# Query-tile order of the last stick-breaking head and of the second sparse group reversed in a two-layer attention trunk

## The chip, the cores and the metric

The kernel runs on one core of a Trainium2 chip (trn2). The metric is device time in microseconds (us), lower is better. The engines are TensorE (PE; its weight loads are PEld), VectorE (DVE), ScalarE (ACT), GpSimd (POOL) and SyncE (SP), which only starts transfers here. POOL and ACT start transfers too.

## The reference, cut to what matters

Two layers, each on 1024 tokens of width 1024. A normalised input goes through one wide projection; two attention mixers read the result; both are gated, projected, merged and added to the residual.

```
h = rms_norm(x, norm_g) * (1 + scale) + shift
sb_q, sb_k, sb_v, sb_z, n_q, k_c, v_c, k_s, v_s, k_w, v_w, n_z, n_g, m_a, m_b = split(h @ w_in)
a = stick_breaking_attention(sb_q, sb_k, sb_v)         # 8 heads, causal
b = native_sparse_attention(...)                       # 8 query heads in 2 groups, causal
a = a * silu(sb_z);  b = b * silu(n_z)
y = sigmoid(m_a) * (a @ w_proj_a) + sigmoid(m_b) * (b @ w_proj_b)
x = x + gate * (y @ w_out)

def stick_breaking_attention(q, k, v):                 # per query tile i of 128 rows
    z = q[tile i] @ k[:tile end].T * scale
    log_keep = where(strict, log_sigmoid(-z), 0)
    between = reverse_cumsum(log_keep) - log_keep
    w = where(strict, exp(log_sigmoid(z) + between), 0)
    out[tile i] = w @ v[:tile end]
...
```

Both mixers are causal, so a query tile near the end of the sequence reads more keys than one near its start.

## The kernel before, in words

Each layer runs four stages: `early` (the first projections), `nsa` (sparse attention), `sb` (stick-breaking attention) and `output`. `nsa` and `sb` work in query tiles `m` = 0 to 3 of 256 tokens; a tile has two halves `x` of 128. Tile `m` of `sb` reads 256m + 128 and 256m + 256 keys in its halves, so tile 0 is the smallest and tile 3 the largest.

`nsa` goes through eight steps `n`: group `g = n // 4`, tile `m = n % 4`. A step has a compressed-branch job and four pair jobs (two head pairs `hp`, two halves `x`). `sb` goes through 32 jobs: eight heads, four tiles each, tiles always from 0 to 3. Each job has a part A (scores and what VectorE and ScalarE make of them: for `sb` two sigmoids into C and E, a running product over C, E times C) and a part B (transposes of E into `tr`, a split into a high and a low half `wh`, `wl`, the products `av` with V, and `merge`). `run_jobs` writes part A of a job between the steps of part B of the job before.

Into these two stages the kernel mixes projection work of its own layer ("fill": 14 groups of 96 matmuls of 512 columns, written by `queue_projections`). `budgets` works out how much of it goes into each slot: what VectorE needs in the slot beyond what TensorE needs, and an equal share of the rest. The tile framework then orders each engine's instructions by the order in the program and by what it takes to be ready, so an instruction of a later stage can stand ahead of one of an earlier stage in an engine's queue.

Transfers around the ends of the stages:

- In the last pair job of a group (`m == 3 and hp == 1 and x == 1`) `nsa` calls `load_kv` for the next group or, after the second, `sb_first`, which writes what is left of the stick-breaking projections and then calls `sb_load(0)` (K by SP into `kk`, q and V by ACT). The buffers of `kk` are shared with the sparse keys, two in all, so the load of K waits for the last scores that read the sparse keys.
- At the end of a job of an odd head, `finish_pair` (L996 to L998) loads the gate rows `szl` (one buffer), multiplies them into the output tile `o` of two heads and stores it from SP to `AD`, rows of that head pair, columns of that tile.
- `output` takes `AD` back in two halves of 512 tokens: half 0 is tiles 0 and 1, half 1 is tiles 2 and 3. `load(half)` starts three transfers per half on POOL (L1462): row blocks 4 to 8 (the sparse heads), 0 to 3 (heads 0 to 5), and 3 to 4 (heads 6 and 7). Each block of 128 rows is then split into `acthi` (ACT, L130) and `actlo` (DVE, L131).
- `load(0)` is written ahead of everything else in `output`. `y_unit` then makes two sums in the two buffers of `proj`: first over blocks 4 to 8, then over 0 to 4, 12 matmuls each, block 3 last. A buffer comes free when VectorE has multiplied it by the gate rows `gt` (L1532), which POOL loads for the first units (L1528). `load(1)` is tied behind the gate loads of the second unit.

The lines that say the order of the first unit:

```
for k0, k1 in ((4, 8), (0, 3), (3, 4)):
    nc.gpsimd.dma_start(lo[:, k0:k1, :].bitcast(F32), self.AD[k0 * P:k1 * P, half * 512:half * 512 + 512]
...
for x, ks in ((1, range(4, 8)), (0, range(0, 4))):
```

Of the kernel before, what the change touches and what calls it, by code (L numbers as in the profile page):

```python
# [87 lines left out]
class Trunk:  # L88
# [186 lines left out]
    def budgets(self):  # L275

        def pe(n):
            return max(0.112, 0.000455 * n)  # L280

        def ve(n):
            return 0.15 + 0.00104 * n

        def parts(nk):
            return [b - a for a, b in self.cuts(nk)]

        def splits(blocks):
            return sum(ve(128 * min(4, blocks - b)) for b in range(0, blocks, 4))

        def nsa(i):
            nk, nw = 128 * i + 128, min(384, 128 * i + 128)
            blocks = (nk + nw) // 64
            A = (4 * (sum(map(pe, parts(nk))) + pe(nw)), 2 * (sum(ve(n) + 0.1 for n in parts(nk)) + ve(nw) + 0.1))
            B = (pe(128) * blocks + 2 * pe(256) * (blocks // 2 + 1),
                 0.34 + 2 * (0.22 + 0.00053 * nk) + splits(blocks) + ve(256) + ve(512) / 2)
            return A, B

        def cmp(m):
            n = 4 * (8 * m + 8)  # L300
            return (8 * pe(128), 2 * (0.5 + 6 * ve(n) + (2.4 if m >= 2 else 0.0))), (4 * pe(128), ve(512))

        def stick(m):
            ks = (256 * m + 128, 256 * m + 256)
            A = (2 * sum(pe(n) for nk in ks for n in parts(nk)) + 0.08, sum(0.13 + 0.0021 * n + ve(n) for n in ks))
            B = (pe(128) * (4 * m + 3) + 2 * (pe(256) * (2 * m + 1) + pe(128)), splits(4 * m + 3) + 1.5 * ve(256))
            return A, B

        seqs = []
        seq = [cmp(0)]  # L310
        for n in range(8):
            i = n % 4 * 2
            seq += [nsa(i), nsa(i + 1)] + ([cmp((n + 1) % 4)] if n < 7 else []) + [nsa(i), nsa(i + 1)]
        seqs.append((seq, 1.25))
        seqs.append(([stick(m) for _ in range(8) for m in range(4)], 1.16))
        zero = ((0.0, 0.0), (0.0, 0.0))
        out = []
        for seq, per in seqs:
            seq = [zero] + seq + [zero]
            out.append([max(0.0, b[1][1] + a[0][1] - b[1][0] - a[0][0]) * per for b, a in zip(seq[:-1], seq[1:])])  # L320
        rest = (14 * 96 * pe(512) - sum(map(sum, out))) / sum(map(len, out))
        return [[(x + rest) * 0.213 / pe(512) for x in o] for o in out]
# [684 lines left out]
        nc.vector.tensor_tensor(o[a:a + 64], ps[a:a + 64, 0:256], t[a:a + 64], ALU.add)  # L1007


    def nsa_load_kv(self, g):  # L1010
        if g < 2:
            pool = self.kvq_pool
            self.kv[g] = (self.load_stack_k(pool, 1536 + g * 64), self.load_stack_k(pool, 1664 + g * 64),
                          self.load_v(pool, 8 + g), self.load_v(pool, 10 + g))
# [15 lines left out]
    def nsa_load_q(self, n):  # L1030
        if n >= 8:
            return
        g, m = n // 4, n % 4
        q = self.tl(self.kvq_pool, [P, 4, 256], F32R, "q")
        for hl in range(2):
            self.nc.scalar.dma_start(
                q[hl * 64:hl * 64 + 64].bitcast(F32),
                self.QK[hl, 1024 + g * 256:1024 + g * 256 + 256, m * 256:m * 256 + 256]
                .rearrange("(h d) t -> d h t", d=64))
        self.qs[n] = q  # L1040
# [17 lines left out]
    def nsa(self, l):  # L1058
        tc, nc = self.tc, self.nc
        with tc.tile_pool(name=f"nsa{l}", bufs=2, reuse_waits="tile") as pool:  # L1060
            kv, qs, cmp = self.kv, self.qs, {}
            load_kv, load_q = self.nsa_load_kv, self.nsa_load_q

            def cmp_job(n):
                g, m = n // 4, n % 4
                st = {"sel": [None, None], "pg": [None, None]}
                cmp[n] = st
                return ([lambda x=x: self.nsa_cmp(pool, g, m, x, qs[n], st) for x in range(2)],
                        [lambda: None] * 2 + [lambda: self.nsa_cmp_t(pool, st)])

            def pair_job(n, hp, x, st):

                g, m = n // 4, n % 4
                hs = {}
                A, B = [], []
                if hp == 0 and x == 0:
                    A.append(lambda: load_q(n + 1))
                if m == 3 and hp == 1 and x == 1:
                    A.append(lambda: load_kv(g + 1) if g == 0 else self.sb_first())
                for r in range(2):  # L1080
                    A += self.nsa_scores(pool, g, m, hp * 2 + r, r, x, lambda: qs[n], lambda: kv[g], cmp[n], hs)
                B.append(lambda: self.nsa_scale(pool, g, m, hp, x, hs))
                B += self.nsa_av(pool, g, m, hp, x, lambda: kv[g], cmp[n], hs)

                def fin():
                    if x == 0:
                        st["o"] = self.tl(pool, [64, 2, 256], F32, "o")
                    self.nsa_merge(pool, hs["ps"], st["o"][:, :, x * P:x * P + P])
                    if x == 1:
                        self.nsa_finish(pool, st["o"], g * 4 + hp * 2, m)  # L1090
                B.append(fin)
                return A, B

            jobs = [cmp_job(0)]
            for n in range(8):
                for hp in range(2):
                    st = {}
                    for x in range(2):
                        if hp == 1 and x == 0 and n + 1 < 8:
                            jobs.append(cmp_job(n + 1))  # L1100
                        jobs.append(pair_job(n, hp, x, st))
            self.run_jobs(jobs, self.budgets()[0])
# [215 lines left out]
    def sb(self, l):  # L1318
        tc, nc = self.tc, self.nc
        with tc.tile_pool(name=f"sb{l}", bufs=2, reuse_waits="tile") as pool:  # L1320
            qkv = self.qkv

            def job(head, m, st):
                hs = {}
                A, B = [], []
                for x in range(2):
                    A += self.sb_scores(pool, m, x, lambda: qkv[head], hs)

                def begin():
                    if m == 0:  # L1330
                        self.sb_load(head + 1)
                    hs["ps"] = self.tl(self.pav, [P, 512], F32, "av", bufs=1)
                bursts = self.pipeline(pool, self.av_stages(pool, m, lambda: (hs["e", 0], hs["e", 1]),
                                                            lambda: qkv[head][2]), lambda: hs["ps"], True)
                B.append(lambda: (begin(), bursts[0]()))
                B += bursts[1:]

                def fin():
                    if head % 2 == 0:
                        st[m] = self.tl(pool, [P, 256], F32, f"o{m}", bufs=1)  # L1340
                    self.merge(pool, hs["ps"], st[m], head % 2)
                    if head % 2 == 1:
                        self.finish_pair(pool, st[m], head // 2 * 128, m, 512 + head // 2 * 128)
                B.append(fin)
                return A, B

            jobs = []
            st = {}
            for head in range(8):
                for m in range(4):  # L1350
                    jobs.append(job(head, m, st))
            self.run_jobs(jobs, self.budgets()[1])

    def sb_scores(self, pool, m, x, qkv, hs):
# [227 lines left out]
```

## Time and profile before

| what | value |
|---|---|
| median of 3 runs | 2152.11 us (2149.16 to 2154.95) |
| the profiled execution | 2147.3 us, span of its records 2145.5 us |
| TensorE busy | 2085.5 us, 97% of the span |
| VectorE busy | 1583.9 us, 74% |
| ScalarE busy | 1125.3 us, 52% |
| mean granted TensorE clock | 0.994 of full speed |
| fill, matmuls of 512 columns per layer | 1344 |

All stretches are in us from the start of the span. Layer 0 has its `nsa` stage at about 284 to 657, `sb` from there to about 911, `output` to about 1150; layer 1 has `nsa` at 1336 to 1703, `sb` to about 1959 and `output` to the end. A wait named "PE tr <- DVE E" is idle time of TensorE in front of a transpose that needed E.

### The profile page before, as it was taken

To read this page: it belongs to the slowest core of one execution; us is meant where nothing else is said; L and a number is where in the kernel's file an instruction comes from. 1 tells how busy PE (TensorE), PEld (TensorE's weight loads), DVE (VectorE), ACT (ScalarE), POOL (GpSimd) and SP (SyncE) were. 2 spreads that over 40 slices of the span, in tenths; PEclk is the share of its full clock that TensorE was granted. 3 is DMA by queue.
4 is the path that set the end of the run, shared out by engine and by line. 5 is a ranking of instruction groups with operands and counts; after the bars stand their busy time and mean duration, and the time that the engine had idled before them with its cause. 6 is when DMAs were issued, how large, how long until landed. Compare 5 with 4: busy or idle time off the path is not lost.

```text
span 2145.5 us, 36387 instructions
## 1 busy us (share of the span) xinstructions
PE 2085.5 (97%) x12952; PEld 1816.3 (85%) x12952; DVE 1583.9 (74%) x3718; ACT 1125.3 (52%) x2461; POOL 59.7 (3%) x218
## 2 busy tenths in 40 slices
PE   4999999999999999999999999999999999999999
PEld 3899788989888878779899987898898888887899
DVE  6758568888887888866766763888888788887543
ACT  5433146666676666653533422656766666666410
POOL 0200000000000000100011000000000000001000
PEclk8999999999999999999999999999999999999999
DMA  8446934243216545365466464322632454535433
GB/s 308 101 146 188 308 101 122 84 131 113 84 55 159 141 119 143 118 221 168 156 163 171 132 193 143 89 95 80 166 102 65 120 131 123 141 99 183 149 123 104
DMA packets 256150, 297.02 MB, mean 138 GB/s; under 512 B 38888, under 2 KB 201568, under 8 KB 255968
## 3 DMA queue, kind: packets, MB, share of 16 engines
q1 hardware_dynamic: 214992, 250.57, 39.1%
q10 hardware_dynamic: 36432, 29.45, 5.3%
q0 software_dynamic: 4544, 14.68, 2.5%
q8 instruction: 102, 1.67, 0.3%
q14 instruction: 80, 0.66, 0.1%
HBM read 206.28 MB, written 83.89 MB: 135 GB/s over the span
## 4 chain that ended last, share of the span: by engine, by line
PE 79%; DVE 8%; DMA 7%; issue 3%; ACT 2%; SPq 1%; POOL 0%; DVEq 0%; ACTq 0%; POOLq 0%
PE proj L182 17%; PE proj L184 17%; PE proj L186 17%; PE tr L969 7%; PE av L989 5%; PE av L988 4%; PE sc L956 4%; PE sc L957 4%; DVE w L131 1%; DVE C L1372 1%; DMA gt<-MD 1%; DMA ada<-in_ada_w 1%; DMA raw<-in_w_in 1%; DVE E L1373 1%; PE sc L1111 1%
## 5 line engine op out<-in xcount | busy, mean ns | idle before, releaser
L182 PE MATMUL proj<-acthi,w 128*128 128x512 f32 x1312 | 533.6, 407 | 5.6 <-DVE gt L1532 3.6
L184 PE MATMUL proj<-actlo,w 128*128 128x512 f32 x1312 | 534.4, 407 | 0.9 <-DVE actlo L131 0.9
L186 PE MATMUL proj<-acthi,w 128*128 128x512 f32 x1312 | 532.5, 406 | 0.0
L130 ACT CAST w<-raw 128x512 fp32r<-128x512 f32 (+1 forms) x296 | 182.2, 622 | 219.8 <-PE proj L186 133.0
L182 PEld LDWEIGHTS proj<-acthi,w 128*128 128x128 f32 x1312 | 248.6, 189 | 46.9 <-DVE gt L1532 4.8
L131 DVE TENSOR_TENSOR wl<-tr,wh 128x512 fp32r<-128x512 f32 (+2 forms) x408 | 253.4, 638 | 46.7 <-ACT wh L130 44.2
L184 PEld LDWEIGHTS proj<-actlo,w 128*128 128x128 f32 x1312 | 248.8, 190 | 38.2 <-DVE actlo L131 2.4
L186 PEld LDWEIGHTS proj<-acthi,w 128*128 128x128 f32 x1312 | 248.2, 189 | 37.8 <-DVE w L131 0.4
L131 DVE TENSOR_TENSOR w<-raw,w 128x512 fp32r<-128x512 f32 (+1 forms) x296 | 202.2, 689 | 83.6 <-ACT w L130 81.5
L130 ACT CAST wh<-tr 128x512 fp32r<-128x512 f32 (+2 forms) x408 | 216.3, 552 | 72.0 <-PE tr L969 65.5
L182 PE MATMUL proj<-w,acthi 128*128 128x256 f32 (+1 forms) x768 | 220.8, 288 | 4.6 <-ACT G L879 2.2
L186 PE MATMUL proj<-w,actlo 128*128 128x256 f32 (+1 forms) x768 | 220.5, 287 | 0.0
L184 PE MATMUL proj<-w,acthi 128*128 128x256 f32 (+1 forms) x768 | 219.6, 286 | 0.1
L988 PE MATMUL av<-wh,V 128*128 128x256 f32 (+1 forms) x776 | 203.7, 280 | 0.4
L989 PE MATMUL av<-wl,V 128*128 128x256 f32 (+1 forms) x776 | 201.2, 287 | 0.9 <-DVE wl L131 0.5
L1372 DVE TENSOR_TENSOR_SCAN C<-C 128x128 f32<-128x128 f32 (+7 forms) x128 | 173.4, 1354 | 24.5 <-ACT C L1368 23.9
L969 PE MATMUL tr<-ident,E 128*128 128x128 f32 x1152 | 180.8, 276 | 9.1 <-DVE E L1373 6.9
L969 PEld LDWEIGHTS tr<-ident,E 128*128 128x128 f32 x1152 | 140.1, 141 | 42.2 <-DVE E L1373 11.9
L956 PE MATMUL sc<-kk,q 128*128 128x384 f32 (+4 forms) x512 | 174.5, 341 | 0.3
L957 PE MATMUL sc<-kk,q 128*128 128x384 f32 (+4 forms) x512 | 172.6, 337 | 0.0
L989 PEld LDWEIGHTS av<-wl,V 128*128 128x128 f32 x776 | 146.0, 188 | 17.3 <-DVE wl L131 7.0
L988 PEld LDWEIGHTS av<-wh,V 128*128 128x128 f32 x776 | 146.5, 189 | 12.2 <-ACT wh L130 4.5
(241 smaller groups left out, 3896.1 us busy)
## 6 DMA issues: line engine op xcount, KB each, us to landing
raw<-in_w_in SPq DMA_DIRECT2D x168, 256.0 KB, 3.3
ada<-in_ada_w SPq DMA_DIRECT2D x48, 512.0 KB, 5.5
kk<-QK SPq DMA_DIRECT2D x48, 512.0 KB, 8.1
q<-QK ACTq DMA_DIRECT2D x64, 256.0 KB, 4.9
QK<-s SPq DMA_DIRECT2D x32, 512.0 KB, 2.8
MD<-sz SPq DMA_DIRECT2D x64, 256.0 KB, 2.3
QK<-s SPq DMA_DIRECT2D x48, 256.0 KB, 4.3
VD<-s SPq DMA_DIRECT2D x48, 256.0 KB, 2.1
```

The costliest lines, as they stand in the source:

```text
L130: nc.scalar.copy(hi, src)
L131: nc.vector.tensor_tensor(lo, src, hi.bitcast(F32), ALU.subtract)
L182: nc.tensor.matmul(ps, lh, rh, start=(x == 0), stop=False)
L184: nc.tensor.matmul(ps, lh, rl, start=False, stop=False)
L186: nc.tensor.matmul(ps, ll, rh, start=False, stop=(x == n - 1))
L956: nc.tensor.matmul(ps, q, k[:, 0, c0:c1], start=True, stop=False)
L957: nc.tensor.matmul(ps, q, k[:, 1, c0:c1], start=False, stop=not masks)
L969: nc.tensor.transpose(pt[:, x * P:x * P + P], b, self.ident)
L988: nc.tensor.matmul(ps[:, c:d], lhsT, hi[:, a:b], start=(first and x == 0), stop=False, skip_group_check=True)
L989: nc.tensor.matmul(ps[:, c:d], lhsT, lo[:, a:b], start=False, stop=(last and x == n - 1), skip_group_check=True)
L1111: nc.tensor.matmul(ps[:, h], q[:, h, x * P:x * P + P], self.KCS[:, :, g * 64:g * 64 + nn], start=True, stop=True)
L1372: nc.vector.tensor_tensor_scan(rev, rev, rev, 1.0, ALU.mult, ALU.bypass)
```

## The change

The second sparse group takes its tiles in the order 3, 2, 1, 0, and the eighth stick-breaking head too; everything else keeps its order. The two functions that say the order are used by the job lists and by `budgets` alike. The call of `load_kv` and `sb_first` stays in the last pair job of each group, which in the second group is now one of tile 0. No instruction is added or removed; jobs, the projection work between them and the transfers tied to them are placed in another order.

```
@@ budgets
         for n in range(8):
-            i = n % 4 * 2
-            seq += [nsa(i), nsa(i + 1)] + ([cmp((n + 1) % 4)] if n < 7 else []) + [nsa(i), nsa(i + 1)]
+            i = self.nsa_at(n)[1] * 2
+            seq += [nsa(i), nsa(i + 1)] + ([cmp(self.nsa_at(n + 1)[1])] if n < 7 else []) + [nsa(i), nsa(i + 1)]
-        seqs.append(([stick(m) for _ in range(8) for m in range(4)], 1.16))
+        seqs.append(([stick(m) for _, m in self.stick_at()], 1.16))
...
+    @staticmethod
+    def nsa_at(n):
+        return (0, n) if n < 4 else (1, 7 - n)
+
+    @staticmethod
+    def stick_at():
+        return [(h, m if h < 7 else 3 - m) for h in range(8) for m in range(4)]
@@ nsa_load_q, cmp_job, pair_job
-        g, m = n // 4, n % 4
+        g, m = self.nsa_at(n)
...
-                if m == 3 and hp == 1 and x == 1:
+                if n % 4 == 3 and hp == 1 and x == 1:
                     A.append(lambda: load_kv(g + 1) if g == 0 else self.sb_first())
@@ sb
-                    if m == 0:
+                    if m == 0 and head < 7:
                         self.sb_load(head + 1)
...
-            for head in range(8):
-                for m in range(4):
-                    jobs.append(job(head, m, st))
+            for head, m in self.stick_at():
+                jobs.append(job(head, m, st))
```

## Rows read from the trace of the kernel before

**Rows 1.** Stretches: length, busy us (instructions) by engine, granted clock, DMA share.
```profile
284.00:640.00 356.00, 355.54 (x2317) 315.39 (x2316) 287.07 (x894) 227.95 (x549) 1.11 (x7) 1.00 0.32 96
640.00:665.00 25.00, 24.94 (x154) 21.12 (x152) 15.57 (x34) 16.39 (x34) 0.73 (x5) 1.00 0.92 222
665.00:880.00 215.00, 212.09 (x1231) 174.57 (x1231) 181.87 (x244) 138.64 (x306) 5.65 (x57) 1.00 0.47 123
...
903.00:917.00 14.00, 11.13 (x62) 8.60 (x61) 12.79 (x22) 9.29 (x18) 3.63 (x6) 1.00 0.88 297
...
1949.50:1953.50 4.00, 1.55 (x9) 1.20 (x7) 3.62 (x6) 3.95 (x9) 0.00 (x0) 0.81 0.52 172
1953.50:1957.00 3.50, 3.50 (x21) 3.27 (x20) 3.35 (x6) 3.18 (x7) 0.00 (x0) 0.73 0.25 75
```

**Rows 2.** TensorE's waits, 900 to 917 (layer 0): us, times, longest.
```profile
PE tr L969 <- DVE E L1373: 1.5, 1, 1.5
PE proj L182 <- DVE gt L1532: 1.0, 1, 1.0
```

**Rows 3.** TensorE's waits, 1945 to 1980 (layer 1).
```profile
PE tr L969 <- DVE E L1373: 2.5, 1, 2.5
PE proj L184 <- DVE actlo L131: 0.9, 3, 0.4
PE proj L182 <- ACT acthi L130: 0.6, 1, 0.6
PE proj L182 <- DVE gt L1532: 0.2, 1, 0.2
```

**Rows 4.** Timeline of VectorE, layer 1: start, us, instruction, idle before it.
```profile
1949.82 0.69 DVE L131 TENSOR_TENSOR actlo<-actlo,acthi 128x512 fp32r<-128x512 f32 x1 [0.81 <-ACT acthi L130]
1950.43 0.68 DVE L131 TENSOR_TENSOR w<-raw,w 128x512 fp32r<-128x512 f32 x1
1951.03 1.22 DVE L1373 TENSOR_TENSOR E<-E,C 128x1024 f32<-128x1024 f32 x1
```

**Rows 5.** Timeline of TensorE at the end of `sb`, layer 1.
```profile
1948.42 0.40 PE L186 MATMUL proj<-acthi,w 128*128 128x512 f32 x1
1948.65 0.39 PE L182 MATMUL proj<-acthi,w 128*128 128x512 f32 x1
...
1952.30 2.61 PE L969 MATMUL tr<-ident,E 128*128 128x128 f32 x11 [2.45 <-DVE E L1373]
```

**Rows 6.** TensorE's timeline: the last product of `sb` in each layer.
```profile
910.69 0.27 PE L989 MATMUL av<-wl,V 128*128 128x128 f32 x1
...
1958.48 0.27 PE L989 MATMUL av<-wl,V 128*128 128x128 f32 x1
```

**Rows 7.** SP's timeline: the last store to `AD` in each layer.
```profile
914.66 0.32 SPq L998 DMA_DIRECT2D AD<-o  x1
...
1961.24 0.32 SPq L998 DMA_DIRECT2D AD<-o  x1
```

**Rows 8.** POOL's timeline: the load of `AD` that needs that store.
```profile
920.32 0.57 POOL L1462 DMA_DIRECT2D actlo<-AD  x1 [11.06 <-DVE w L131]
...
1966.80 0.57 POOL L1462 DMA_DIRECT2D actlo<-AD  x1 [4.23 <-issue]
```

**Rows 9.** Lines L998 (32 stores) and L1462 (12 loads): issue to landing.
```profile
DMA to landing us min/median/max: 1.7/3.0/5.5
...
DMA to landing us min/median/max: 5.2/8.6/11.0
```

**Rows 10.** DMA issues by size, section 6 and its longer answer: KB, median us to landing.
```profile
kk<-QK SPq DMA_DIRECT2D x48, 512.0 KB, 8.1
...
AD<-o SPq DMA_DIRECT2D x64, 128.0 KB, 2.5
...
actlo<-AD POOLq DMA_DIRECT2D x4, 256.0 KB, 6.9
```

**Rows 11.** Timelines of SP and TensorE, layer 0: first K load, first score of `sb`.
```profile
643.12 0.57 SPq L937 DMA_DIRECT2D kk<-QK  x1
...
652.55 0.23 PE L956 MATMUL sc<-kk,q 128*128 128x128 f32 x1
```

More of the change, by code (lines that the diff above doesn't have):

```diff
@@ L1064, in cmp_job @@
             def cmp_job(n):
-                g, m = n // 4, n % 4
+                g, m = self.nsa_at(n)
                 st = {"sel": [None, None], "pg": [None, None]}
@@ L1071, in pair_job @@
             def pair_job(n, hp, x, st):
-                g, m = n // 4, n % 4
+                g, m = self.nsa_at(n)
                 hs = {}
```

## The prediction

> **What bounds the kernel now.** I read the busy times by stretch first, then TensorE's waits in the stretches where it was not full, then the timelines of the engines at the two stage ends, and last the landing times of the transfers there.
>
> The stretches say that TensorE sets the pace almost everywhere: in the sparse stage of layer 0 it is busy 355.54 of 356 us, and in the 25 us across the change of stage, from sparse to stick-breaking, 24.94 of 25 [rows 1]. In the body of the stick-breaking stage it loses about 3 of 215 us [rows 1]. So reordering jobs inside these stages can win next to nothing there: the same matmuls run, and the projection work already fills the gaps. What there is to win lies where TensorE stands still. At the end of the stick-breaking stage of layer 0 it waits 1.5 us for the last E, and 2.5 us in layer 1 [rows 2, 3]. The reader should see why the second is longer: VectorE, which takes its queue in order, first waits 0.81 us for a block that `output` has loaded, splits it, splits a weight block, and only then multiplies the last, 1024 wide E [rows 4].
>
> The clock makes the second wait dearer. It is granted at 0.81 in 1949.5 to 1953.5 and at 0.73 in 1953.5 to 1957 [rows 1]. A loss of 0.19 over 4 us and of 0.27 over 3.5 us is 1.5 and 1.9 us at the lower of the two levels, 1.2 GHz instead of 2.4, together 3.4 us. TensorE starts again at 1952.30 with 11 transposes that take 2.61 us [rows 5]; about 3.1 of the 3.4 us lie behind that start, so about 1.5 us of work is lost. Before the fall it had stood still. In layer 0, where it stood for 1.5 us, the clock stayed at 1.00 [rows 1, 2].
>
> **The change, part by part.** No instruction is added or dropped; three things move.
>
> *The last jobs of the stick-breaking stage become small.* The last E is 256 wide, not 1024, and its part B has 3 transposes and 6 products, not 15 and 30. This takes away the waits for E: 1.5 + 2.5, and the 1.5 of the clock, 5.5 us in both layers together. The splits of the loaded blocks still stand in VectorE's queue around the last E, so I leave 0.5 us per layer and count −4.5 (ends: 0, if those splits hold up the small E as well, and −5.5). By the formula in `budgets` the last two slots hold 25.7 + 2.4 matmuls of fill before and 9.3 + 4.3 after; the sum over the stages is the same, so this is work moved and not saved.
>
> *The half that `output` needs first is now finished last.* This is the part that costs. Tiles 0 and 1 of heads 6 and 7 are block 3 of half 0. Before, half 1 was the late half, and `output` needs it later. The trace has the whole late chain, for half 1. From the end of the last product, 910.96 and 1958.75 [rows 6], to the store on SP it is 3.7 and 2.5 us [rows 7]: a copy, an addition and the gate product. From the store to the POOL load that needs it, another 5.7 and 5.6 us [rows 8]. Over all 32 stores the landing takes 1.7 to 5.5, median 3.0 [rows 9]. The load of this size takes 6.9 at the median, and no load of that line under 5.2 [rows 9, 10]. Then come the two splits, 0.7 each by the one in [rows 4] (ACT's estimated alike).
>
> For half 0 I take 2.5 to the store, 3.0 to its landing (the median, because the 1.75 MB of the other half need not be in the queues then), 6.0 for the load (between 5.2 and 6.9) and 1.4 for the splits: 12.9 us from the last product until block 3 can be used. Ends: 2.5 + 1.7 + 5.2 + 1.4 = 10.8, and 3.7 + 5.7 + 6.9 + 1.4 = 17.7.
>
> What hides it is the work of `y_unit` without block 3: 12 + 9 matmuls in the first unit. They follow each other every 0.23 us [rows 5], so 4.9 us. The two `proj` buffers allow as many in the second unit, if the engines' queues are written so that it goes ahead; then both buffers hold sums that want block 3 and TensorE must stop. That gives 9.8 us. Some 9 matmuls (2.1 us) will run beside the last small job, an estimate from its 2.5 us of transposes, split and products. So 7.7 us lie behind the last product, or 2.8 if only the first unit is there. The queues do mix later work in (the block split ahead of E in [rows 4] is one case), so I take 7.7: the stall is 12.9 − 7.7 = 5.2 us. It is longer than the one after which the clock fell in layer 1, so I add 1.5 for the clock. Per layer 6.7, for both 13.4 (ends: 3.1 without the clock, 6.2 for both; 17.7 − 2.8 + 1.5 = 16.4, 32.8 for both).
>
> The waits now at the head of `output` fall into this stall: 1.0 for `gt` in layer 0, and 0.9 + 0.6 + 0.2 in layer 1 [rows 2, 3]: −2.7 (ends 0 and −2.7). What queues behind the late load: on POOL it is in front of whatever follows it, which may be the `gt` loads; on ACT and DVE the splits of block 3 are in front of later gate products. If `gt` is caught too, the cover is the 2.8 us.
>
> The Trainium skill, page "DMA: Bandwidth & Descriptors", section "Anatomy of one DMA — SWDGE (gpsimd) path", says that a transfer takes about 2.0 us plus its bytes at 436 GB/s, the first part mostly waiting until the last write is confirmed. Estimated from that page, 128 KB [rows 10] would take 2.3 us and 256 KB 2.6, the chain 2.5 + 2.3 + 2.6 + 1.4 = 8.8, the stall 1.1 a layer without a fall of the clock, and the whole sum −3.0. The trace disagrees for the load, whose shortest is 5.2 [rows 9].
>
> *The sparse stage ends with tile 0.* K of the first stick-breaking head can be loaded only once the last sparse scores are done. Before, 9.4 us passed from that load, 643.12, to the first score, 652.55, with part B of a large job in between and hardly any idle time [rows 1, 11]. Now part B of the last job is small: 8 transposes and 10 products, about 2 us. With the second half's remaining window scores and products and the fill of the slots there (about 5 + 8.4 + 8.5 matmuls by `budgets`, 5.1 us), TensorE has 7 to 9 us of work, against 8.1 us for the landing of a K transfer [rows 10]. More fill can be drawn ahead, but what is drawn there is missing later. I count 1.0 us per layer, +2.0 (ends 0 and 2.4 per layer, which is 9.4 − 7). The order 3, 3, 2, 1 in the middle of the stage costs nothing: TensorE is full there with every size of job [rows 1]; without that cover, as in the stick-breaking body, it would be of the order of 1 us in 70.
>
> **The sum** against the profiled execution: −4.5 − 2.7 + 13.4 + 2.0 = +8.2 us. Its span is 2145.5 us, about 2 us less than its own time and about 7 below the median of the runs; laid on the median of 2152.1 the sum gives 2160. A measurement here tells about 0.3%, 6.5 us, from no change.
>
> **The rivals.**
>
> *The late block is nearly hidden.* If store and load run at their shortest and the second unit goes ahead, the stall is 3.1 a layer without the clock: −4.5 − 2.7 + 6.2 + 2.0 = +1, 2153. For it: the queues carry less when half 1 is not asked for at the same time. Against it: the store that ends the stage took 5.6 us and more in both layers [rows 7, 8]. The page's rule above, with 2149, belongs here.
>
> *The change does nothing that counts.* TensorE is full in the stages [rows 1], and gains and losses at the ends cancel: within 4 us of 2152. The gains for it are in [rows 2, 3]; against it speaks that block 3 of half 0 must come later by construction.
>
> *Faster.* The waits all go, −5.5 − 2.7 = −8.2, and nothing comes in their place: 2144. This is decided at one place: block 3 of half 0 must be usable within 7.7 us of the last product. The shortest pieces in the trace give 10.8, so it needs a load well under 5.2.
>
> *Much slower.* The `gt` loads stand behind the late load on POOL. Then the cover is 2.8, the stall 10.1 + 1.5 a layer, and the sum −4.5 − 2.7 + 23.2 + 2.0 = +18, 2170.
>
> **How the numbers follow.** The forecast has 0.40, much slower 0.12, the nearly hidden block 0.25, the cancelling 0.15, faster 0.08. Slower by over 0.3% (above 2158.6) are the first two, 0.52; within 0.3% the next two, 0.40; faster 0.08. The predicted time is 2160. The range goes from 2148, below the nearly hidden case and most of the cancelling one, to 2172, above the much slower one; outside I leave the faster case and the tail of the long chain, under 2 in 10. The forecast's own range is 2156 to 2166.
>
> **What would show it.** Right: the wait of transposes for E at the end of the stick-breaking stage falls under 1 us in both layers; in its place a wait of 3 us or more of `proj` matmuls for `acthi` or `actlo`, some 3 to 10 us behind the last product; the third load of half 0 on POOL starts 5 us or more after the last product; the clock is below 1.00 in the stretch that follows. Around the K load a wait of scores of 0 to 2.4 us. Wrong: no wait of `proj` for block 3, which would mean that the chain is short or that other work was put in front of it; or a wait for E that stays.

## The result and the profile after

The changed kernel takes 2175.71 us (median of 4 runs, 2169.27 to 2181.55), the kernel before 2151.74 in the runs beside it. The ratio is 1.0116, with a 95% interval from 1.0100 to 1.0131. So the change costs 24.0 us, where 8.2 were forecast; the time lies above the range. The profiled execution takes 2175.72 us and the one of before 2147.3; in this pair the difference is 28.4 us.

The page of the changed kernel, its part on busy times:

```profile
span 2173.9 us, 36400 instructions
...
PE 2095.1 (96%) x12952; PEld 1823.6 (84%) x12952; DVE 1582.7 (73%) x3718; ACT 1125.8 (52%) x2461; POOL 59.0 (3%) x218
```

TensorE runs the same 12952 matmuls. Its idle time is the span less its busy time, 78.8 us where it was 60.0: 18.8 of the 28.4 us. The other 9.6 are busy time of the same matmuls, for which the clock can account: summed over the clock records of both traces, it stood at 1.2 GHz for 55.2 us, and for 24.9 before.

Where the time comes in is seen when the same instruction is looked up in TensorE's timeline of both kernels:

| start of | before | after | later by | added since the row above |
|---|---|---|---|---|
| sparse stage, layer 0 | 283.73 | 286.26 | 2.53 | 2.53 |
| its last product of the compressed branch | 656.16 | 663.00 | 6.84 | 4.31 |
| last product of `sb`, layer 0 | 910.69 | 920.68 | 9.99 | 3.15 |
| first product with `w_out`, layer 0 | 959.28 | 978.20 | 18.92 | 8.93 |
| sparse stage, layer 1 | 1334.93 | 1352.78 | 17.85 | −1.07 |
| its last product of the compressed branch | 1702.36 | 1722.71 | 20.35 | 2.50 |
| last product of `sb`, layer 1 | 1958.48 | 1980.40 | 21.92 | 1.57 |
| first product with `w_out`, layer 1 | 2051.01 | 2079.42 | 28.41 | 6.49 |

The first 2.53 us lie ahead of any changed instruction; they are difference between two executions, as this row stands at 285.21 to 290.21 in the traces of the twelve kernels below. Some of the second row is of that kind too: in a kernel whose sparse stages are those of before (the one with the splits tied behind the last E, below) the same stretch takes 374.02 us, 1.6 more than in the kernel before. More than half of the rest, 8.93 + 6.49 = 15.4 us, comes in at the head of `output`, in the sums of `y_unit`. That is the place that the prediction named.

TensorE's waits in the changed kernel around that place, first layer 0 (890 to 960), then layer 1 (1940 to 2010):

```profile
PE proj L182 <- ACT acthi L130: 6.6, 1, 6.6
PE proj L182 <- DVE gt L1541: 2.3, 1, 2.3
PE av L988 <- ACT wh L130: 1.7, 1, 1.7
PE av L989 <- DVE wl L131: 1.3, 2, 1.1
```

```profile
PE proj L182 <- ACT acthi L130: 6.7, 1, 6.7
PE av L988 <- ACT wh L130: 1.7, 1, 1.7
PE av L989 <- DVE wl L131: 1.3, 2, 1.1
```

Against [rows 2, 3]: the waits for E, 1.5 and 2.5, are gone. In their place stand a wait of 6.6 and 6.7 for the split of a loaded block, and two small ones inside the last jobs, for the two halves of the split weights, 3.0 in each layer. The wait for gate rows did not vanish in layer 0, it grew from 1.0 to 2.3.

The clock in the same stretches of the changed kernel, beside those of the change of stage (the columns are those of [rows 1]):

```profile
640.00:665.00 25.00, 25.00 (x152) 21.41 (x151) 17.00 (x56) 16.75 (x49) 0.63 (x4) 1.00 0.51 133
...
917.00:935.00 18.00, 11.44 (x43) 8.83 (x43) 7.94 (x15) 5.03 (x11) 4.75 (x8) 0.78 0.46 141
1949.50:1953.50 4.00, 3.74 (x23) 2.98 (x21) 2.46 (x4) 1.29 (x4) 0.10 (x1) 1.00 0.00 0
...
1982.00:1990.00 8.00, 2.92 (x13) 2.03 (x11) 2.25 (x5) 0.00 (x0) 2.15 (x4) 0.85 0.38 121
1990.00:1994.00 4.00, 2.41 (x5) 1.62 (x6) 1.38 (x2) 1.50 (x3) 2.60 (x5) 0.50 0.82 254
```

In 1982 to 1990 TensorE works 2.92 of 8 us, and behind that, in 1990 to 1994, the clock granted is 0.50, the lower level. At 1949.5 to 1953.5, where the kernel before stood still [rows 1], the changed one is in the middle of its job and full.

Now the late chain of layer 0, piece by piece. TensorE's timeline: the first and the last matmul of the first `y_unit` without block 3, the last product of `sb` between them, and the matmul that had to wait.

```profile
919.69 0.39 PE L182 MATMUL proj<-acthi,w 128*128 128x512 f32 x1
...
920.68 0.27 PE L989 MATMUL av<-wl,V 128*128 128x128 f32 x1
...
924.79 0.40 PE L186 MATMUL proj<-acthi,w 128*128 128x512 f32 x1
931.75 0.79 PE L182 MATMUL proj<-acthi,w 128*128 128x512 f32 x1 [6.56 <-ACT acthi L130]
```

The timelines of the engines that carry the chain, in the same stretch:

```profile
921.40 0.44 SPq L996 DMA_DIRECT2D szl<-SZ  x1
...
924.13 0.42 DVE L997 TENSOR_TENSOR o<-o,szl 128x256 f32<-128x256 f32 x1
...
924.58 0.40 SPq L998 DMA_DIRECT2D AD<-o  x1
...
928.04 0.57 POOL L1471 DMA_DIRECT2D actlo<-AD  x1 [21.23 <-DMA AD<-o]
928.62 2.13 POOL L1537 DMA_DIRECT2D gt<-MD  x4
...
931.08 0.62 ACT L130 CAST acthi<-actlo 128x512 fp32r<-128x512 f32 x1 [9.15 <-DMA actlo<-AD]
...
934.86 1.30 ACT L1539 ACTIVATE gt<-gt 128x512 f32<-128x512 f32 x2 [2.46 <-DMA gt<-MD]
```

From the end of the last product, 920.95, the chain is 3.6 us to the store, 3.5 to the load that needs it, 3.0 to the split, 0.7 until TensorE starts: 10.8 in all (layer 1: from 1980.67 to 1991.59, 10.9). In front of it TensorE has only 18 of the 21 matmuls left, until 925.19: a cover of 4.2 us. The POOL load stands at the head of its queue for 21.23 us, and the four gate loads and then `load(1)` begin right behind it, at 928.62 and after. ACT then waits 2.46 us for gate rows, and behind it TensorE waits 2.3.

The load of 256 KB took 3.0 us here, with the 16 DMA engines at a share of 0.46 in 917 to 935; the shortest of its line before was 5.2 [rows 9]. The Trainium skill, page "DMA: Bandwidth & Descriptors", section "Anatomy of one DMA — SWDGE (gpsimd) path", gives 2.6 us by its fit (an estimate from that page); for this load the trace agrees within 0.4. That section of the Trainium skill gives the fit for transfers that POOL starts; the store of 128 KB is started by SP, and the trace has 2.9 us from its issue to its landing and 3.5 to the load that waited for it.

### The profile page after: what moved, and what is told of

It is laid out like the page before. It is cut to its first block, busy times and chain, and to the rows that moved or that the text cites. A ratio compares the mean times of both kernels' runs of the same rounds, so it can differ in the third digit from the quotient of the medians.

```text
span 2173.9 us, 36400 instructions
## 1 busy us (share of the span) xinstructions
PE 2095.1 (96%) x12952; PEld 1823.6 (84%) x12952; DVE 1582.7 (73%) x3718; ACT 1125.8 (52%) x2461; POOL 59.0 (3%) x218
## 4 chain that ended last, share of the span: by engine, by line
PE 78%; DVE 8%; DMA 7%; issue 4%; ACT 2%; SPq 0%; POOL 0%; ACTq 0%; DVEq 0%; POOLq 0%
PE proj L182 17%; PE proj L186 17%; PE proj L184 17%; PE tr L969 7%; PE av L989 4%; PE av L988 4%; PE sc L956 4%; PE sc L957 4%; DVE C L1381 2%; DMA V<-VD 1%; DMA ada<-in_ada_w 1%; DVE w L131 1%; DVE wl L131 1%; DMA actlo<-AD 1%; DVE E L1382 1%
## 5 line engine op out<-in xcount | busy, mean ns | idle before, releaser
L956 PE MATMUL sc<-kk,q 128*128 128x512 f32 (+4 forms) x512 | 175.2, 342 | 0.2
L957 PE MATMUL sc<-kk,q 128*128 128x512 f32 (+4 forms) x512 | 173.7, 340 | 0.0
```

The source lines that it names most:

```text
L956: nc.tensor.matmul(ps, q, k[:, 0, c0:c1], start=True, stop=False)
L957: nc.tensor.matmul(ps, q, k[:, 1, c0:c1], start=False, stop=not masks)
```

## The experiments

The theory: block 3 of half 0 is complete last, and TensorE waits for it at the head of `output`. Its rivals: the fallen clock behind the stall is a good part of the loss; what stands in POOL's queue makes the loss, not the block; the small last jobs cost by themselves; the sparse group's new order costs at the change of stage.

Times are medians, ratios are to the kernel before on the same chip, each with its 95% interval. Diffs are against the changed kernel, but where the text says otherwise.

**Either half of the change alone.** First the stick-breaking head only:

```diff
 def nsa_at(n):
-    return (0, n) if n < 4 else (1, 7 - n)
+    return n // 4, n % 4
```

> Only the eighth stick-breaking head is reversed; the second sparse group keeps the order 0 to 3. Theory A, the late block: most of the loss is that block 3 of half 0 comes last, with the gate loads queued behind it on POOL. In the changed kernel the stretch from the last product of the stick-breaking stage to the first output matmul grew by 8.9 us in layer 0 and 6.5 us in layer 1, and the stage before it by 1 to 3, so the time should be 14 to 20 us above before (ratio 1.007 to 1.009), with two waits of proj matmuls for acthi of 6 to 7 us. Theory B, the change of stage from sparse to stick-breaking: this kernel should be within 6 us of before. Theory C, both alike: about 12 us above before.

Measured: 2165.42 us, 1.0077 [1.0058, 1.0095], +16.6 us. TensorE's waits at the head of `output`, layer 1:

```profile
PE proj L182 <- ACT acthi L130: 7.0, 1, 7.0
```

In layer 0 the same wait is 6.7; with the sparse group alone (the next run) no wait for `acthi` at this place is over 0.7. So the late block comes with the reversed head. The stage itself became a little shorter, in one execution: from the last product of the compressed branch to the last product of `sb` it takes 253.95 and 254.30 us, against 254.52 and 256.12 before, with two fill matmuls more in it. The head of `output` takes this back and more. Then the sparse group only:

```diff
 def stick_at():
-    return [(h, m if h < 7 else 3 - m) for h in range(8) for m in range(4)]
+    return [(h, m) for h in range(8) for m in range(4)]
```

> Only the second sparse group is reversed; the heads keep their order. Theory A: 4 to 9 us above before, from the wait of av products for V (2.2 and 3.6 us in the changed kernel), the half clock behind it (about 1.7 us a layer) and nothing at the end of the stick-breaking stage. Theory B: 15 us or more above before. Theory C: about 12 us above.

Measured: 2155.86 us, 1.0028 [1.0017, 1.0040], +6.0 us. So the reversed group has a price of its own; the two parts together, 1.0105, make up the whole change, 1.0116, within their intervals. Its wait stands behind the change of stage, in layer 0 (640 to 700):

```profile
PE av L988 <- DMA V<-VD: 3.1, 1, 3.1
```

It is V, not K. In layer 1 of this run no wait for V stands, so V is no more than a part of the 6.0. K of the first head is asked for at 654.91 in the changed kernel instead of 643.12 [rows 11], and its first score at 663.57 does not wait. But now the K loads of two heads and V fall together. Two windows of before and the same two of after:

```profile
655.00:665.00 10.00, 9.96 (x54) 7.98 (x52) 3.39 (x8) 4.22 (x10) 0.73 (x5) 1.00 1.08 261
665.00:676.00 11.00, 10.27 (x55) 7.89 (x55) 10.22 (x14) 7.26 (x17) 0.50 (x5) 1.00 0.07 28
```

```profile
655.00:665.00 10.00, 10.00 (x60) 8.40 (x60) 5.95 (x18) 5.94 (x15) 0.63 (x4) 1.00 1.01 256
665.00:676.00 11.00, 8.89 (x43) 6.82 (x41) 5.10 (x9) 6.46 (x14) 0.29 (x3) 1.00 1.11 260
```

Before, the DMA engines were done by 665 (share 0.07 in the second window); now they are full until 676 (1.11). V, issued on ACT at 663.08, took 12.9 us to land, where the V loads of this stretch took 5.1 to 9.2 before. That loads of several queues share the same 16 engines is also what the Trainium skill says ("Trainium Kernel Development and Optimization", section "Key Constraints"), and the trace agrees: V from ACT takes longer where K loads from SP are under way and the share is at 1.11.

**The late block taken away.** Block 3 of half 0 is loaded from the rows of block 2, which are stored early; the kernel leaves out the rows of heads 6 and 7 there and the wait for their store:

```diff
-self.AD[k0 * P:k1 * P, ...]
+s0 = 2 if half == 0 and k0 == 3 else k0
+self.AD[s0 * P:(s0 + k1 - k0) * P, ...]
```

> The changed kernel, but block 3 of half 0 is loaded from the rows of block 2 (heads 4 and 5), which were stored long before; the output is made from the wrong rows there, all instructions and sizes stay. This takes away the wait for the last store and nothing else. Theory A: 10 to 16 us below the changed kernel, so 8 to 14 above before; no wait of proj matmuls for acthi over 1 us, the third POOL load right behind the first two, the clock at 1.00 after the last product. Theory B, or a theory that the loss lies in the transfers of half 1 or the smaller jobs themselves: within 4 us of the changed kernel.

Measured: 2158.54 us, 1.0045 [1.0027, 1.0062], against 1.0116 for the whole change: 0.0071 of 2152, so 15.3 us (about 5 either way, by the two intervals), is the lateness of this one block with what queues behind it. TensorE's waits, layer 0:

```profile
PE proj L182 <- DVE gt L1542: 4.6, 1, 4.6
PE av L988 <- ACT wh L130: 1.6, 1, 1.6
PE av L989 <- DVE wl L131: 1.3, 2, 1.1
```

No wait for `acthi` is left, but the small last jobs still wait for their weights and the gate rows are waited for longer than before [rows 2]. The gains that were to come with the small jobs do not show even when the late block is gone.

**Was the wait for E worth anything?** Two kernels. In the first, the last head takes 0, 1, 3, 2, in which both halves keep their order and the last E is smaller:

```diff
-    return [(h, m if h < 7 else 3 - m) for h in range(8) for m in range(4)]
+    return [(h, m if h < 7 else (0, 1, 3, 2)[m]) for h in range(8) for m in range(4)]
```

(with the sparse group as before)

> The kernel before, but the eighth stick-breaking head takes its tiles in the order 0, 1, 3, 2, so the stage ends with the second largest job and half 0 is as early as before. Theory A: no late block, so within 3 us of before, with the waits for the last E (1.5 and 2.5 us) shorter by up to 1 us each and the half clock of layer 1 perhaps gone: 0 to 4 us below before. Rival: any other order than 0 to 3 costs something by itself (the largest jobs of two heads closer together, VectorE late): 3 us or more above before.

Measured: 2153.46 us, 1.0025 [1.0014, 1.0036], about 5 us above before: not faster, and where its rival had it. The wait for E fell to 0.8 in both layers and one of 2.8 for `actlo` came in layer 0. So an order other than 0 to 3 has a price without any late block; what makes it up beyond that wait was not followed. In the second, the kernel before keeps its order, and the splits of the loaded blocks are tied behind the last E on VectorE and ACT:

```diff
...
 for f in load(0):
-    f()
+    with tc.issue_after(self.e_last.ins):
+        f()
```

> The kernel before, with nothing reversed; only the splits of the loaded blocks of half 0 are tied behind the last product E times C in VectorE's queue, which stood behind one of them and a weight split. If the wait for the last E (1.5 and 2.5 us) comes from that order and not from the size of the last job, it falls by 1 to 2 us a layer and the half clock of layer 1 goes: 2 to 5 us below before. Rival, the size: the wait stays within 0.5 us, and the time within 1 us of before.

Measured: 2149.09 us, 0.9996 [0.9987, 1.0006]. Layer 1, 1940 to 2015:

```profile
PE av L988 <- DVE actlo L131: 2.6, 1, 2.6
...
PE tr L969 <- DVE E L1373: 0.6, 1, 0.6
```

The wait for E shrinks from 2.5 to 0.6, and the products behind it wait 2.6 for what VectorE put off. The clock stays at 1.00 in 1950 to 1962, where it fell before [rows 1]. The time stays as well, and the interval leaves out the −4.5 us of the forecast (0.9979). So one wait was exchanged for another, and what stands behind is as late; neither the wait for E nor the fallen clock behind it had a price that shows. What a wait is worth that goes with nothing in its place, this run does not tell.

**What could shorten the stall.** Four edits of the changed kernel, one link each. The gate loads on SP instead of POOL:

```diff
-self.gt = (nc.gpsimd if ku < 2 else nc.sync).dma_start(
+self.gt = nc.sync.dma_start(
```

> The changed kernel, but the gate rows gt of the first units are loaded by SP instead of POOL, so they no longer stand behind the late load of block 3. Theory A1, the wait itself: what counts is TensorE's own wait for block 3, which stays at 6 to 7 us a layer; only the wait for gt behind it (2.3 us) goes, so 2 to 6 us below the changed kernel, 18 to 22 above before. Theory A2, the queue: the gate loads behind the late load are the larger part; then TensorE goes on with the second unit and the kernel is 10 us or more below the changed one.

Measured: 2179.66 us, 1.0136 [1.0121, 1.0151], no gain: the interval still touches that of the change, and the wait got longer. The timelines of POOL and SP:

```profile
919.03 2.06 POOL L1471 DMA_DIRECT2D actlo<-AD  x3 [11.48 <-PE proj L186]
931.77 0.55 POOL L1471 DMA_DIRECT2D actlo<-AD  x1 [10.68 <-DMA AD<-o]
```

```profile
920.83 0.97 SPq L996 DMA_DIRECT2D szl<-SZ  x1
...
929.45 0.34 SPq L998 DMA_DIRECT2D AD<-o  x1
```

Three loads of `load(1)` (919.03) got ahead of the late load. In their traffic (DMA share 0.97 in 921 to 929) the gate row `szl` of the last store took 8.1 us to land, the store went out at 929.45 instead of 924.58, and the wait for `acthi` grew to 12.5 in both layers. So the short chain of the changed kernel rests on queues that hold little else. Next, the late load behind the first unit's gate loads on POOL:

```diff
-for k0, k1 in ((4, 8), (0, 3), (3, 4)):
+for k0, k1 in ((4, 8), (0, 3), (3, 4))[part]:
...
+if ku == 0 and x == 0 and half == 0:
+    with self.tc.issue_after(self.gt.ins):
+        self.late()
```

> The changed kernel, but the load and the split of block 3 of half 0 are written behind the gate loads of the first unit, so on POOL two gate loads stand ahead of the late load and not behind it. Theory F, POOL's order: the gates are there when block 3 comes, the wait for gt behind it (2.3 us in layer 0) goes and the products of the first unit leave their buffers at once: 4 to 8 us below the changed kernel. Rival: the transfers that start only behind the late load (half 1, the second unit's gates) set the pace in any case: within 3 us of the changed kernel, with a wait for acthi of 6 to 7 us a layer as before.

Measured: 2171.51 us, 1.0109 [1.0096, 1.0122]. TensorE's timeline, layer 0:

```profile
924.71 0.50 PE L182 MATMUL proj<-acthi,w 128*128 128x512 f32 x1 [0.50 <-DVE gt L1545]
925.05 0.40 PE L184 MATMUL proj<-actlo,w 128*128 128x512 f32 x1
931.05 0.79 PE L182 MATMUL proj<-acthi,w 128*128 128x512 f32 x1 [5.60 <-ACT acthi L130]
```

Two gate loads now start at 917.65, and the wait for the block is 5.6 and 5.2. By the ratios 1.5 us are won back, and the interval overlaps that of the change. A buffer comes free early now (924.71, behind a gate product), but only two matmuls of the second unit stand ahead of the first unit's last three on TensorE; gate rows that are there early cover next to nothing. Two buffers for the gate rows of the last store, so that its row can be loaded earlier:

```diff
-sz = self.tl(pool, [P, 256], F32, "szl", bufs=1)
+sz = self.tl(pool, [P, 256], F32, "szl2", bufs=2)
```

> The changed kernel, but the gate rows szl of the stick-breaking stage have two buffers, so those of the last job are loaded while the job before is still multiplying. In the changed kernel the last product ends at 920.95, the addition behind it at 922.69 and the gate product starts only at 924.13: 1.4 us for the gate rows. The store, the late load and everything behind them should come 1.4 us earlier in each layer: 2 to 4 us below the changed kernel. Rival: the landing of the store and the load take it up: within 1 us.

Measured: 2171.43 us, 1.0108 [1.0095, 1.0121]; waits 6.0 and 6.1, 0.6 shorter each. Again no difference that the intervals tell from the change. Last, the clock: 26 matmuls of 512 columns, whose sums nobody reads, fill the wait.

```diff
...
+for _ in range(26):
+    nc.tensor.matmul(idle, w[2][:, 0, 0, 0:P], ab[half][0][:, 4, :], start=True, stop=True)
```

> The changed kernel, but while TensorE would wait for block 3 of half 0 it runs 26 matmuls of 512 columns into a score buffer that nobody reads (6.1 us at the full clock), in both layers. The work of no use costs nothing if it fits into the wait. Theory D, the clock: the half clock behind the wait (6.8 to 10.2 us a layer at 1.2 GHz in the changed kernel, which loses half of what TensorE works in it) is a part of the loss of its own; then the kernel is 4 to 9 us below the changed one and the granted clock behind the last product is 1.00. Rival: the output stage waits for transfers there anyway, so the clock costs nothing: within 2 us of the changed kernel.

Measured: 2174.80 us, 1.0118 [1.0101, 1.0134]. TensorE's timeline, layer 0:

```profile
926.52 6.23 PE L1547 MATMUL sc<-acthi,w 128*128 128x512 f32 x26
933.64 0.50 PE L182 MATMUL proj<-acthi,w 128*128 128x512 f32 x1 [0.90 <-ACT acthi L130]
```

The stall is filled, the clock granted is 1.00 in 928 to 940, the clock records hold 42.4 us at the lower level instead of 55.2, and the time is the same. Behind the block TensorE waits 4.0 us for gate rows in layer 0 (2.3 before the filling). The theory that the fallen clock was 4 to 9 us of the loss is not borne out: there the next transfer would have been waited for anyway. The two intervals together leave room for about 4 us, so a smaller part is not ruled out.

**A third buffer for V**, with the sparse group alone reversed:

```diff
-v = self.tl(pool, [P, NT, P], F32R, "V")
+v = self.tl(pool, [P, NT, P], F32R, "V", bufs=3)
```

> The kernel with only the second sparse group reversed, but with three buffers of V instead of two, so V of the first stick-breaking head can be loaded before the last sparse products have read theirs. Theory E: the group alone costs because V comes late: the wait of av products for V (3.1 us in layer 0) and the half clock with it go, and the kernel is within 3 us of before. Rival: the loss of 6 us has another place (the wait for K, the fill drawn ahead, the clock at the start of the sparse stage): 4 us or more above before, with the wait for V gone all the same.

Measured: 2152.16 us, 1.0012 [1.0002, 1.0022], 3.5 us under the reversed group alone, and no wait for V. But the intervals overlap, and V was issued no earlier (664.22, against 662.84 without the third buffer); it was in use 11.6 us later, against 14.7. Whether the buffer did it stays open.

**Does the order of the halves explain it?** The reversed head alone, with `output`, and the stages of the next layer behind it, taking half 1 first:

```diff
...
-for f in load(0):
+for f in load(1):
...
-for halves in ([(0, 1)] if last else [(0,), (1,)]):
+for halves in ([(1, 0)] if last else [(1,), (0,)]):
```

> Only the eighth head is reversed, and the output stage takes half 1 (tiles 2 and 3) first and half 0 second, in both layers; the next layer starts with half 1 too. The half that is finished last is then the half that is needed last, as in the kernel before. Theory A, the late block: the 16.6 us that the reversed head cost go; within 4 us of before, with no wait of proj matmuls for acthi over 1.5 us behind the last product. If the small last job is worth something by itself, it shows here: 2 to 5 us below before. Rival: a stage that ends with small jobs costs by itself (part B of the last jobs waits on short chains): 6 us or more above before.

Measured: 2158.96 us, 1.0052 [1.0040, 1.0064]. Waits for `acthi` of 8.3 and 7.2 stay. POOL and TensorE, layer 0:

```profile
911.09 2.09 POOL L1471 DMA_DIRECT2D actlo<-AD  x3 [11.99 <-PE proj L184]
```

```profile
911.84 0.28 PE L989 MATMUL av<-wl,V 128*128 128x128 f32 x1
920.45 0.80 PE L182 MATMUL proj<-acthi,w 128*128 128x512 f32 x1 [8.34 <-ACT acthi L130]
```

This is another wait under the same name. POOL waited 11.99 us for a fill matmul, the last reader of the buffer in which half 1 lands; the first blocks were loaded from 911.09 on, and TensorE had nothing at all to do from 912. The fill ends with half 1. So the fill was turned round as well:

```diff
 for u in range(2):
-    for half in range(2):
+    for half in (1, 0):
```

> The stick-breaking part of the change alone, with the output stage taking half 1 before half 0 as in the run before, and with the projection fill taking half 1 before half 0 too, so that the buffers of half 1, in which the block of the output stage lands, are free one unit of 24 matmuls earlier. Theory A (the stage ends with the half that the output stage needs first, and that alone costs): now the half that comes first is complete as early as in the kernel before, so the waits of 6 to 8 us for its last block go; at most 1 us of them stays per layer, and the run is within 4 us of before (ratio 0.998 to 1.002). Rival (the small jobs at the end of the stage cost by themselves, by less work that covers the load, whichever half comes first): waits of 3 us or more for blocks of half 1 or for the last store stay in both layers, and the ratio is above 1.004.

Measured: 2155.50 us, 1.0028 [1.0017, 1.0039] (12 runs). TensorE's waits, layer 0 and layer 1:

```profile
PE proj L182 <- DVE gt L1541: 5.7, 1, 5.7
...
PE proj L184 <- DVE actlo L131: 3.3, 3, 2.8
PE proj L182 <- DVE gt L1541: 1.6, 1, 1.6
...
PE proj L182 <- ACT acthi L130: 0.7, 1, 0.7
```

The waits of 6 to 8 us for `acthi` are gone, and the ratio of the reversed head goes from 1.0077 to 1.0028. That is neither the 1.002 of the one theory nor the 1.004 of the other. About two thirds of the head's cost go with the order of the halves, in the output stage and in the fill. The rest may be the waits that now stand there, 5.7 for gate rows in layer 0 and 3.3 for `actlo` in layer 1; why these come was not tried. Nor was the kernel before with its halves and fill turned round, so what that order does by itself is not known.

No kernel of these was faster than the one before.

## Why the prediction was wrong

The direction, the place and the mechanism of the loss were right: slower, at the head of `output`, by a wait for block 3 of half 0, with a fallen clock behind it. The sum was 8.2 and 24.0 was measured. The step that failed most is the one that counted the waits that go as time won (−4.5 and −2.7): they went, and no time was won. The cover of the stall and the price of the sparse group's order were mis-sized as well. Term by term, from differences of ratios, each good to about 5 us either way or less:

- *Gains, −4.5 and −2.7.* The waits for E did go as said, and the time did not. The kernel that takes them out of the order of before is at 0.9996. With the late block taken out and the reversed group's 6.0 us set aside, the small jobs come to 1.0045 − 1.0028 = 0.0017, +3.7 us. That kernel has no stall for the old waits to fall into, so its +3.7 stands against −4.5 alone. The intervals of the two ratios are about as wide as this difference: its sign is less sure than that 4.5 us were not gained. The waits of a small job for its split weights, 3.0 us a layer, and the longer wait for gate rows stand in the trace; that they make up the price, no run shows. Of the −2.7, layer 1's part went, and the wait for `gt` in layer 0 grew from 1.0 to 2.3.
- *Late block, +13.4.* The kernel with the early block puts it at +15.3, which holds the old waits too, so it stands against 13.4 − 2.7 = 10.7. That the stall came out near, 6.6 and 6.7 where 5.2 was forecast, is luck: two errors cancelled. The chain was 10.8 us (3.6 to the store, 3.5 landing, 3.0 load, 0.7 split, where 2.5 + 3.0 + 6.0 + 1.4 stood), above all since the load was quick. The cover was 4.2 us, not 7.7, and that is the step that failed here. The second unit was to go ahead "if the engines' queues are written so that it goes ahead". They are not: the gate loads that free a `proj` buffer stand behind the late load on POOL (928.62), and with the gates early only two matmuls of the second unit stand ahead of the three that want block 3. The first unit alone gave 4.2 and not 2.8, as 3 of its 21 matmuls and not 9 ran beside the last job.
- *Change of stage, +2.0.* The reversed group measured +6.0. K came in time, as the lower end had it; the wait that was forecast for scores did not show. In the changed kernel V was late instead, by 2.2 and 3.6 us, where loads that were spread before now meet. The text priced the moved K loads, and not what is queued in the DMA engines behind them.

With measured terms the sum is 15.3 + 3.7 + 6.0 = 25.0, and 24.0 was measured.

One reading of the rows was wrong too. The 5.7 and 5.6 us of [rows 8] are no time of the store: POOL's load is released there by VectorE's `w` in layer 0 and by nothing that the profile shows in layer 1, so they are upper bounds. In the changed kernel, where the store does release the load, it is 3.5 and 3.4. The sum took 3.0 and did not need them; the upper end and the argument against the nearly hidden block did.

The rival "much slower" came closest in number. It had the gate loads behind the late load right, but its stall of 10.1 is 3.5 too long, and it kept the gains of 7.2; that its 2170 is near is luck. Undoing its one link won 1.5 us, within the intervals: the block's own chain comes first, and what is behind it only follows.

"What would show it": the wait for E under 1 us, the wait for `acthi` over 3, the POOL load over 5 us behind the last product (7.1), the clock under 1.00 behind it: all seen. A wait for K was given as 0 to 2.4, and is 0.

Open: how much of V's lateness a third buffer cures, and what else the group's order costs. That `sb` takes 3.15 us longer in layer 0, although it holds 10 fill matmuls fewer, comes with the sparse group: alone it makes this stretch 3.2 us longer, with the wait for V in it, and the reversed head alone makes it 0.6 shorter. The 1.57 of layer 1 is not explained: alone, both parts make the stretch shorter there, by 1.3 and 1.8 us.

## What to carry to other kernels

A wait at the end of a stage is a gain only if what stands behind it on the path is earlier; try that first, by moving the work that causes the wait, before an order is turned round for it. Before jobs are reordered, ask which output tiles the next stage reads first and whose buffers come free last: both ends of the order, producer and consumer, and the fill between them, have to agree. And count as cover only what stands ahead of the waiting instruction in its own engine's queue; a free buffer behind it is none.

## What was not expected of the hardware

A load of 256 KB that found the 16 engines at a share of about 0.5 was used 3.0 us after its issue, where 12 loads of that line before took 5.2 at the least; V took 12.9 us with the 16 engines full (share 1.11). And 12.8 us less at 1.2 GHz (55.2 to 42.4) were worth nothing measurable (1.0116 against 1.0118); in layer 0 TensorE then waited 4.0 us for gate rows in place of 2.3.
